# Queue order of expert weights, halved loads and a regrouped end in a two-layer mixture-of-experts kernel

## The chip, the cores and the metric

One core of a Trainium2 chip (trn2) runs the whole program. The metric is the device time of one execution in microseconds (us); of several executions the median counts. PE is the matrix engine (TensorE), DVE the vector engine, ACT the scalar engine, SP the engine whose only task here is to issue transfers (DMAs) from memory to the on-chip buffers.

## What is computed

Two decoder layers on 256 tokens of width 1024, all in float32. Each layer is a mixer (layer 0: sparse attention beside block attention; layer 1: stick-breaking attention), a layer norm, a mixture of 16 experts, and a second layer norm. The change touches the experts alone:

```python
def hierarchical_moe(x, w_grp, b_grp, w_rt, b_rt, w_gate, w_up, w_down):
    ...                      # two experts for each token, weights in combine
    def per_sequence(args):
        xs, cs = args
        h = jax.nn.silu(jnp.einsum('sd,edf->sef', xs, w_gate)) * jnp.einsum('sd,edf->sef', xs, w_up)
        return jnp.einsum('sef,efd->sd', h * cs[..., None].astype(h.dtype), w_down)
    return lax.map(per_sequence, (x, combine))

def reference(x, ...):
    for layer in range(DEPTH):
        ...
        x = layer_norm(DEEPNORM_ALPHA * x + mix, ln_mix_g[layer], ln_mix_b[layer])
        ffn = hierarchical_moe(x, ...)
        x = layer_norm(DEEPNORM_ALPHA * x + ffn, ln_ffn_g[layer], ln_ffn_b[layer])
    return x
```

An expert has 2 MB of gate and up weights (1024 x 512) and 1 MB of down weights (256 x 1024), so a layer reads 48 MB of expert weights.

## The kernel before

The 16 experts of a layer are worked through in seven units: `POS = [(0, 1), (2, 3), (4, 5), (6, 7), (16,), (8, 9, 10, 11), (12, 13, 14, 15)]`. Units 0 to 3 are pairs of experts with 64 token slots each, unit 4 takes overflow tokens, units 5 and 6 are four experts with 32 slots each. Places from 6 on are filled by the token counts at run time, and their weights are fetched by a register address (`expert`, a load of a register on SP the first time a place is asked for).

A unit passes through these steps, each a function: `gather(u)` picks its tokens into `xg` (L1201), `gate_up(u)` multiplies them with the gate and up weights, 8 chunks of 128 rows by 2 or 4 experts (L1234), `act_h` applies silu on ACT and the product on DVE (L1240, L1242), `tr_h` transposes the result on PE (L1249) and copies it to `hT` on ACT (L1250), `down(u)` multiplies with the down weights, two column halves of 512 (L1266), and splits each half into a high part (ACT, L190) and a low part (DVE, L198), and `scatter(u)` adds the rows back to the tokens in four accumulators `oacc[t][h]` (L1275). `scatter_end` (L1281) does the last scatters of units 5 and 6. The four experts of units 5 and 6 stand in four row strips ("lanes") of the matrix engine, so four products run side by side; each product of the program is two rows in the trace.

The steps of neighbouring units overlap; the order of the calls at the end of `moe_` is written by hand, and a scheduler that orders by its own estimates decides how the products of overlapping steps interleave on an engine. Each engine then works strictly in that order. `tc.issue_after(x)` tells the scheduler to place what follows behind instruction x.

Weights come through SP's one queue, in program order. A load at the head that waits for its buffer holds back all loads behind it. A load also waits until the eighth load before it has landed, since eight semaphores take turns. The buffers:

- six of 2 MB (`wtile`, pool `wp`) in rotation, for gate and up weights, mixer weights, and one pair of down weights (`w2`);
- four of 1 MB (`wd_tile`) in rotation for down weights;
- one of 1 MB (`wd_extra`), used for expert 4, then for the first expert of unit 5, then for the last expert of unit 6.

`load_gu(l, q)` loads the pair q as two loads, each four chunks of both experts; `load_gu_of(u, j)` loads piece j of a unit, one load for each expert; `load_d_at` and `load_d_of` load the 1 MB of down weights of one expert. After the last of them, in layer 0, come `wb` (2 MB of the next mixer's weights, L76) and the rows of gain and bias of the layer norm, `lngb` (two loads of 512 KB, L307).

The end of layer 0 is a layer norm by token halves t = 0, 1 (`ln_tile`): sums on DVE (L319, L321), the product with the gain on DVE (L347, needs the first `lngb`), two squares on ACT (L328), the root (L331 to L335), the last product (L356), transposes on PE (L284), copies to `xT` on ACT (L291), and then the first products of the next mixer, 16 rows for each half (L229). Thirty small products (L302) keep the matrix engine busy from the last scatter on.

## Time and profile before

| | us |
|---|---|
| median of 3 runs (539.48 to 541.42) | 541.22 |
| the profiled execution | 538.35 |
| its span, first to last instruction | 536.6 |
| PE busy | 503.1 |
| ACT busy | 221.9 |
| DVE busy | 289.4 |

The profiled execution is 2.9 us below the median of the three runs. What lies around its span is 1.75 us. The experts of layer 0 run from about 165 us to 276 us, those of layer 1 from about 412 us to 523 us, and the layer norm that ends the program follows. A sum over a stage has to be read in that stage: the matrix engine is busy 94% of the span, but the two ends of the expert stages hold most of what is left.

### The profile page before, as it was taken

To read this page: it belongs to the slowest core of one execution; us is meant where nothing else is said; L and a number is where in the kernel's file an instruction comes from. 1 tells how busy PE (TensorE), PEld (TensorE's weight loads), DVE (VectorE), ACT (ScalarE), POOL (GpSimd) and SP (SyncE) were. 2 spreads that over 40 slices of the span, in tenths; PEclk is the share of its full clock that TensorE was granted. 3 is DMA by queue.
4 is the path that set the end of the run, shared out by engine and by line. 5 is a ranking of instruction groups with operands and counts; after the bars stand their busy time and mean duration, and the time that the engine had idled before them with its cause. 6 is when DMAs were issued, how large, how long until landed. Compare 5 with 4: busy or idle time off the path is not lost.

```text
span 536.6 us, 8446 instructions
## 1 busy us (share of the span) xinstructions
PE 503.1 (94%) x3170; PEld 317.5 (59%) x3170; DVE 289.4 (54%) x828; ACT 221.9 (41%) x425; POOL 6.6 (1%) x18
## 2 busy tenths in 40 slices
PE   6998989999999999999989999999999999999980
PEld 3886666666676354543354997798677544363330
DVE  5587986957759732221158364555748861141116
ACT  5383635547647021221146237665847421131022
POOL 0000000000001000000000000000002000000000
PEclk9799989999999999999999999999999999999896
DMA  8999500007967899999998790002985599999952
GB/s 265 350 428 434 206 1 1 0 1 277 427 238 307 337 366 340 410 423 420 434 425 379 302 368 37 1 1 101 425 318 225 221 393 340 409 422 420 425 223 84
DMA packets 25247, 150.01 MB, mean 280 GB/s; under 512 B 3440, under 2 KB 3824, under 8 KB 14704
## 3 DMA queue, kind: packets, MB, share of 16 engines
q1 hardware_dynamic: 25200, 149.41, 69.8%
q8 instruction: 27, 0.44, 0.3%
q14 instruction: 20, 0.16, 0.1%
HBM read 148.35 MB, written 1.05 MB: 278 GB/s over the span
## 4 chain that ended last, share of the span: by engine, by line
PE 81%; DVE 8%; DMA 5%; ACT 4%; issue 1%; SPq 0%; ACTq 0%; DVEq 0%
PE pmt L1234 15%; PE pmt L1266 8%; PE pmt L1201 4%; PE acc L221 4%; DMA wb<-w1s 4%; PE acc L220 3%; PE acc L219 3%; PE acc L1275 3%; PE acc L373 3%; PE acc L371 3%; PE acc L372 3%; PE acc L229 3%; PE acc L243 2%; PE acc L241 2%; PE acc L242 2%; PE z L850 2%
## 5 line engine op out<-in xcount | busy, mean ns | idle before, releaser
L1234 PE MATMUL pmt<-wgu,xg 128*64 128x512 f32 (+1 forms) x512 | 93.5, 599 | 0.0
L193 DVE TENSOR_TENSOR wl<-wb,wh 128x512 fp32r<-128x512 f32 (+1 forms) x78 | 49.1, 661 | 22.4 <-ACT wh L190 22.3
L190 ACT ACTIVATE wh<-wb 128x1024 fp32r<-128x1024 f32 (+2 forms) x41 | 40.9, 1000 | 45.3 <-PE acc L220 21.3
L1234 PEld LDWEIGHTS pmt<-wgu,xg 128*64 128x64 f32 (+1 forms) x512 | 27.3, 124 | 53.5 <-issue 50.8
L1266 PE MATMUL pmt<-wd,hT 128*64 128x512 f32 (+1 forms) x256 | 54.6, 604 | 0.9 <-ACT hT L1250 0.9
L219 PE MATMUL acc<-wh,xhl 128*128 128x512 f32 (+1 forms) x112 | 45.9, 410 | 4.0 <-ACT wh L190 3.3
L221 PE MATMUL acc<-wl,xhl 128*128 128x512 f32 (+1 forms) x112 | 45.7, 414 | 3.2 <-DVE wl L193 3.2
L220 PE MATMUL acc<-wh,xhl 128*128 128x512 f32 (+1 forms) x112 | 45.1, 402 | 0.0
L198 DVE TENSOR_TENSOR yl<-pmt,yh 128x512 fp32r<-128x512 f32 x20 | 13.8, 690 | 49.1 <-ACT yh L190 49.1
L1242 DVE SCALAR_TENSOR_TENSOR hh<-pmt,cs,silu 128x256 f32<-128x256 f32 x12 | 5.8, 484 | 56.8 <-ACT silu L1240 56.8
L1240 ACT ACTIVATE silu<-pmt 128x256 f32<-128x256 f32 x12 | 4.6, 384 | 76.1 <-PE pmt L1234 76.1
L190 ACT ACTIVATE yh<-pmt 128x512 fp32r<-128x512 f32 x20 | 11.9, 597 | 57.5 <-PE pmt L1266 57.5
L1266 PEld LDWEIGHTS pmt<-wd,hT 128*64 128x64 f32 (+1 forms) x256 | 15.4, 124 | 27.2 <-issue 25.3
L221 PEld LDWEIGHTS acc<-wl,xhl 128*128 128x128 f32 x112 | 22.2, 199 | 9.3 <-DVE wl L193 4.0
L219 PEld LDWEIGHTS acc<-wh,xhl 128*128 128x128 f32 x112 | 22.4, 200 | 8.9 <-ACT wh L190 4.4
L1201 PEld LDWEIGHTS pmt<-Poh,xhl 128*128 128x128 f32 x192 | 24.5, 188 | 5.3 <-issue 3.2
L241 PE MATMUL acc<-xhl,wh 128*128 128x256 f32 x96 | 27.6, 287 | 0.0
L1201 PE MATMUL pmt<-Poh,xhl 128*128 128x256 f32 (+1 forms) x192 | 26.8, 293 | 0.3 <-DVE xg L1209 0.3
L243 PE MATMUL acc<-xhl,wl 128*128 128x256 f32 x96 | 27.0, 281 | 0.0
L242 PE MATMUL acc<-xhl,wh 128*128 128x256 f32 x96 | 26.8, 280 | 0.0
L373 PE MATMUL acc<-xol,oT 128*128 128x512 f32 x64 | 26.1, 412 | 0.0
L371 PE MATMUL acc<-xo,oT 128*128 128x512 f32 x64 | 25.9, 410 | 0.0
(367 smaller groups left out, 964.3 us busy)
## 6 DMA issues: line engine op xcount, KB each, us to landing
wd<-wd SPq DMA_DIRECT2D x34, 1024.0 KB, 11.0
wgu<-wgu SPq DMA_DIRECT2D x64, 512.0 KB, 11.6
wgu<-wgu SPq DMA_DIRECT2D x14, 2048.0 KB, 10.4
wb<-w1s SPq DMA_DIRECT2D x6, 2048.0 KB, 19.6
wo<-wo SPq DMA_DIRECT2D x4, 2048.0 KB, 16.9
wgu<-wgu SPq DMA_DIRECT2D x8, 1024.0 KB, 6.9
wb<-w SPq DMA_DIRECT2D x3, 2048.0 KB, 19.4
wb<-w SPq DMA_DIRECT2D x2, 1024.0 KB, 12.2
```

What stands on the lines that cost most here:

```text
L190: A.activation(dst_h, src, AF.Copy)
L193: V.tensor_tensor(dst_l[:, i], src[:, i], dst_h[:, i].bitcast(F32), OP.subtract)
L219: PE.matmul(a[t][:, :n], xh[:, cc, ts], wh[:, c, :n], start=(cc == 0), stop=False)
L220: PE.matmul(a[t][:, :n], xl[:, cc, ts], wh[:, c, :n], start=False, stop=False)
L221: PE.matmul(a[t][:, :n], xh[:, cc, ts], wl[:, c, :n], start=False, stop=(cc == NCH - 1))
L241: PE.matmul(o, wh[:, c, fs], xh[:, cc], start=(cc == 0 and f % 2 == 0), stop=False, skip_group_check=True)
L243: PE.matmul(o, wl[:, c, fs], xh[:, cc], start=False, stop=(cc == NCH - 1), skip_group_check=True)
L371: PE.matmul(a[t][h], oc[:, 0, ts], wh[:, hs], start=first, stop=False)
L373: PE.matmul(a[t][h], oc[:, 0, ts], wl[:, hs], start=False, stop=last)
L1201: PE.matmul(p[:, 0:w], src[:, t, c * 128:c * 128 + 128], P[:, t, u * 128:u * 128 + w], start=(t == 0 and src is xh), stop=(t == 1 and src ...
L1234: PE.matmul(pg[r, :], g[:, c, BASE[u] + r.start:BASE[u] + r.stop], ws[k, c], start=(c == 0), stop=(c == NCH - 1), tile_position=(0, r.start))
L1266: PE.matmul(y[r, :], hT[:, fc, r], wd[k][:, fc, h * 512:h * 512 + 512], start=(fc == 0), stop=(fc == 1), tile_position=(0, r.start))
```

## The change

Four edits, the same in both layers, since `moe_` is called for each.

1. The third pair (experts 4 and 5) is loaded by `load_gu(l, 2)`: two loads of four chunks of both experts, in place of one load for each expert. The down weights of expert 4 follow both.
2. `load_gu_of(5, 0)`, four loads of 512 KB, goes ahead of the down weights `load_d_at(2, 1)` and `load_d_of(3, 0)`.
3. The down weights of unit 6 are loaded by column halves: the first 512 columns of experts 0 to 3, then the last 512 columns of 0 to 3. The buffers are the same, and the last expert's is still `wd_extra`.
4. The scatters of unit 5 that stand at the end are placed behind the last gate product of unit 6, the last scatters of unit 6 behind its last down product, and their order is changed.

```diff
         weights, Am, seconds = router(lg)
         load_gu(l, 1)
-        wloads[l, 2, 0] = {}
-        for i in range(2):
-            w = chunks(wtile("wgu"))
-            SP.dma_start(w, io["wgu"][l * NE + 4 + i])
-            for c in range(NCH):
-                wloads[l, 2, 0][i, c] = w[:, c]
-            if i == 0:
-                load_d_at(2, 0, wd_extra())
+        load_gu(l, 2)
+        load_d_at(2, 0, wd_extra())
...
+        def load_d_half(u, i, wd, h):
+            hs = slice(h * 512, h * 512 + 512)
+            SP.dma_start(wd[:, :, hs], io["wd"][l * NE:(l + 1) * NE][ds(expert(POS[u][i]), 1)].rearrange("e p (f n) -> p (e f) n", f=2)[:, :, hs])
+            wloads.setdefault((l, u, 1), {})[i] = wd
...
-        def scatter_end(u1, u2):
-            for u, h, t in ((u2, 0, 0), (u1, 0, 1), (u1, 1, 1), (u2, 1, 0), (u2, 0, 1), (u2, 1, 1)):
-                for i in range(2):
-                    last["PE"] = PE.matmul(oacc[t][h], ...)
+        def scatter_end(u1, u2, down2):
+            for u, h, t in ((u1, 0, 1), (u1, 1, 1), (u2, 0, 0), (u2, 1, 0), (u2, 0, 1), (u2, 1, 1)):
+                with (tc.issue_after(down2) if u == u2 else nullcontext()):
+                    for i in range(2):
+                        last["PE"] = PE.matmul(oacc[t][h], ...)
...
         do_down(0)
+        load_gu_of(5, 0)
         load_d_at(2, 1, wd_tile())
         load_d_of(3, 0, wd_tile())
-        load_gu_of(5, 0)
...
-        load_d_of(6, 0, w2[:, 0])
-        load_d_of(6, 1, w2[:, 1])
+        w6 = [w2[:, 0], w2[:, 1]]
+        load_d_half(6, 0, w6[0], 0)
+        load_d_half(6, 1, w6[1], 0)
...
-        load_d_of(6, 2, wd_tile())
+        w6.append(wd_tile())
+        load_d_half(6, 2, w6[2], 0)
...
-        load_d_of(6, 3, wd_extra())
+        w6.append(wd_extra())
+        load_d_half(6, 3, w6[3], 0)
+        for i in range(4):
+            load_d_half(6, i, w6[i], 1)
...
         hid[6], _ = act_h(6, pg)
+        gate6 = last["G"]
         do_tr(6)
-        do_scatter(5, [0])
+        with tc.issue_after(gate6):
+            do_scatter(5, [0])
...
-        scatter_end(5, 6)
+        with tc.issue_after(gate6):
+            scatter_end(5, 6, last["D"])
```

Here `last["G"]` and `last["D"]` are the latest gate product and down product. What the scheduler makes of it shows in the order of the instructions on the engines. Line numbers of the changed kernel differ by a few (L1233 is L1234 of before, L1265 is L1266, L1274 is L1275, L1248 is L1249).

On PE at the end of the experts, the rows from the last down products of unit 5 (`pmt<-wd,hT`) on; `pmt<-wgu,xg` are gate products of unit 6, `acc<-yh,ST` and `acc<-yl,ST` scatters of unit 5, `pmt<-identf,hh` the transposes of unit 6. Before:

```order
L1266 MATMUL pmt<-wd,hT 32x512 x12
L1234 MATMUL pmt<-wgu,xg 32x512
L1275 MATMUL acc<-yh,ST 128x512
L1275 MATMUL acc<-yl,ST 128x512
L1234 MATMUL pmt<-wgu,xg 32x512
L1275 MATMUL acc<-yh,ST 128x512
L1275 MATMUL acc<-yl,ST 128x512
L1281 MATMUL acc<-yh,ST 128x512
L1281 MATMUL acc<-yl,ST 128x512
L1281 MATMUL acc<-yh,ST 128x512
L1281 MATMUL acc<-yl,ST 128x512
L1234 MATMUL pmt<-wgu,xg 32x512 x14
```

and in the changed kernel:

```order
L1265 MATMUL pmt<-wd,hT 32x512 x12
L1233 MATMUL pmt<-wgu,xg 32x512 x16
L1274 MATMUL acc<-yh,ST 128x512
L1274 MATMUL acc<-yl,ST 128x512
L1274 MATMUL acc<-yh,ST 128x512
L1274 MATMUL acc<-yl,ST 128x512
L1281 MATMUL acc<-yh,ST 128x512
L1248 MATMUL pmt<-identf,hh 128x128 x2
L1281 MATMUL acc<-yl,ST 128x512
L1281 MATMUL acc<-yh,ST 128x512
L1281 MATMUL acc<-yl,ST 128x512
L1265 MATMUL pmt<-wd,hT 32x512 x16
```

The 16 gate products now follow the down products without a scatter between them, and the eight scatters stand between the gates and unit 6's down products, the transposes among them; the count of each kind is the same.

On ACT in the layer norm that ends layer 0, from the root of the first token half (L332) on; `acc,lnst<-xn,lnst` is a square of one column half, `xT<-pmt` the copies of the first token half's transposes. Before:

```order
L332 ACTIVATE lnst<-lnst 128x1
L291 ACTIVATE xT<-pmt 128x4x128 x2
L328 ACTIVATE acc,lnst<-xn,lnst 128x512 x2
L331 ACTIVATE lnst<-lnst 128x1
L332 ACTIVATE lnst<-lnst 128x1
L190 ACTIVATE xhl<-xT 128x4x128 x2
```

and in the changed kernel:

```order
L332 ACTIVATE lnst<-lnst 128x1
L328 ACTIVATE acc,lnst<-xn,lnst 128x512
L291 ACTIVATE xT<-pmt 128x4x128 x2
L328 ACTIVATE acc,lnst<-xn,lnst 128x512
L331 ACTIVATE lnst<-lnst 128x1
L332 ACTIVATE lnst<-lnst 128x1
L190 ACTIVATE xhl<-xT 128x4x128 x2
```

The first square of the second token half has moved ahead of the two copies of the first token half. In layer 1 ACT's order is that of before, and DVE's is in both layers.

On SP at the end of layer 0's expert loads, from the last loads of unit 6 on (`ISA`, which sets the register address, stands ahead of each). Before:

```order
L1182 ISA
L1182 DMA wd<-wd 128x2048
L76 DMA wb<-w1s 128x4096
L307 DMA lngb<-lng 128x1024
L307 DMA lngb<-lnb 128x1024
```

and in the changed kernel (the first `wd` row here is the first half of the last expert, into `wd_extra`; three first halves stand ahead of it):

```order
L1181 DMA wd<-wd 128x2x512
L1181 ISA
L1181 DMA wd<-wd 128x2x512
L1181 ISA
L1181 DMA wd<-wd 128x2x512
L1181 ISA
L1181 DMA wd<-wd 128x2x512
L1181 ISA
L1181 DMA wd<-wd 128x2x512
L76 DMA wb<-w1s 128x4096
L307 DMA lngb<-lng 128x1024
L307 DMA lngb<-lnb 128x1024
```

Behind the load into `wd_extra` there now stand four more halves before `wb` and the rows of the layer norm.

## Rows read from the trace of the kernel before

**Rows 1.** The page: span, busy times, the DMA engines' busy tenths in 40 slices of 13.4 us, and the chain that ended last, by engine.

```profile
span 536.6 us, 8446 instructions
PE 503.1 (94%) x3170; PEld 317.5 (59%) x3170; DVE 289.4 (54%) x828; ACT 221.9 (41%) x425; POOL 6.6 (1%) x18
DMA  8999500007967899999998790002985599999952
PE 81%; DVE 8%; DMA 5%; ACT 4%; issue 1%; SPq 0%; ACTq 0%; DVEq 0%
```

**Rows 2.** PE in order of time, end of the experts of layer 1: start, duration (us), line, operation, number of rows in the trace, and in brackets the idle time before and what ended it. The first row is the first scatter behind unit 5's down products.

```profile
508.11 0.50 PE L1275 MATMUL acc<-yh,ST 128*128 128x512 f32 x1
...
509.15 1.05 PE L1234 MATMUL pmt<-wgu,xg 128*32 128x512 f32 x2
...
511.72 3.63 PE L1234 MATMUL pmt<-wgu,xg 128*32 128x512 f32 x28
516.35 0.44 PE L1249 MATMUL pmt<-identf,hh 128*128 128x128 f32 x2 [1.00 <-DVE hh L1242]
517.26 3.68 PE L1266 MATMUL pmt<-wd,hT 128*32 128x512 f32 x32 [0.47 <-ACT hT L1250]
520.87 2.37 PE L1281 MATMUL acc<-yb,ST 128*128 128x512 f32 x8
```

**Rows 3.** The same of layer 0, with the first products of the next mixer.

```profile
260.81 0.50 PE L1275 MATMUL acc<-yh,ST 128*128 128x512 f32 x1
...
264.42 3.63 PE L1234 MATMUL pmt<-wgu,xg 128*32 128x512 f32 x28
...
269.96 3.68 PE L1266 MATMUL pmt<-wd,hT 128*32 128x512 f32 x32 [0.47 <-ACT hT L1250]
...
280.61 1.13 PE L284 MATMUL pmt<-identf,xn 128*128 128x128 f32 x8
281.90 7.13 PE L229 MATMUL acc<-wb,xT 128*128 128x512 f32 x16 [0.15 <-ACT xT L291]
```

**Rows 4.** Waits of the issuing engine SP: what waited, for what, us in total, times, longest. First row: from 186 to 204 us (layer 0, the down weights of expert 5 at the head). Second: from 246 to 262 us (layer 0, the load into `wd_extra`). Third: from 493 to 509 us (the same of layer 1).

```profile
SPq L1015 <- PE pmt L1266: 7.8, 1, 7.8
...
SPq L1182 <- PE pmt L1266: 5.8, 1, 5.8
...
SPq L1182 <- PE pmt L1266: 5.1, 1, 5.1
```

**Rows 5.** Stretches: from:to and length (us), busy time and count of PE, PE weight load, DVE, ACT, POOL, then the granted clock as a share, the DMA engines' busy share and GB/s. In the last row only the output's rows of 2 KB are under way; in the fourth, pieces of 4 and 8 KB.

```profile
192.00:193.00 1.00, 1.00 (x10) 1.00 (x9) 0.67 (x2) 0.33 (x2) 0.00 (x0) 1.00 0.76 156
...
195.90:250.60 54.70, 53.24 (x348) 24.55 (x347) 12.03 (x30) 10.18 (x22) 0.00 (x0) 1.00 1.00 393
...
444.00:494.90 50.90, 50.64 (x348) 23.86 (x347) 11.41 (x29) 9.32 (x20) 0.00 (x0) 1.00 1.01 397
...
462.00:482.00 20.00, 19.74 (x161) 11.06 (x156) 6.28 (x15) 4.96 (x11) 0.00 (x0) 1.00 1.02 423
...
531.00:532.00 1.00, 0.00 (x0) 0.00 (x0) 0.90 (x2) 0.00 (x0) 0.00 (x0) 0.50 1.01 391
```

**Rows 6.** Single loads: start and duration of the issue on SP, and below it KB and us from issue to landing. First pair: the load into `wd_extra` of layer 0; second: the gain of the layer norm that ends layer 0; third: the load into `wd_extra` of layer 1. The last three rows are loads issued while no other load was outstanding, at 423.98, 370.79 and 313.73 us.

```profile
260.10 0.33 SPq L1182 DMA_DIRECT2D wd<-wd  x1
wd<-wd SPq DMA_DIRECT2D x1, 1024.0 KB, 8.9
261.01 0.37 SPq L307 DMA_DIRECT2D lngb<-lng  x1
lngb<-lng SPq DMA_DIRECT2D x1, 512.0 KB, 14.1
507.40 0.33 SPq L1182 DMA_DIRECT2D wd<-wd  x1
wd<-wd SPq DMA_DIRECT2D x1, 1024.0 KB, 9.7
wgu<-wgu SPq DMA_DIRECT2D x1, 1024.0 KB, 5.2
wd<-wd SPq DMA_DIRECT2D x1, 1024.0 KB, 4.8
wgu<-wgu SPq DMA_DIRECT2D x1, 2048.0 KB, 8.7
```

**Rows 7.** DVE and ACT in order of time in the layer norm that ends layer 0: the product with the gain (first token half), the sum of the second token half, then on ACT the copies to `xT` of the first token half and the first square of the second.

```profile
276.70 1.28 DVE L347 SCALAR_TENSOR_TENSOR lnu<-xn,lnst,lngb 128x1024 f32<-128x1024 f32 x1
...
282.22 0.21 DVE L321 TENSOR_SCALAR lnst<-lnst 128x1 f32<-128x1 f32 x1
...
281.25 1.13 ACT L291 ACTIVATE xT<-pmt 128x512 f32<-128x512 f32 x2 [2.31 <-DMA wb<-w1s]
282.47 0.69 ACT L328 ACTIVATE acc<-xn,lnst 128x512 f32<-128x512 f32 x1
```

**Rows 8.** Stretches again, columns as in rows 5: unit 5's down products with unit 6's gate products in layer 0, the same in layer 1, and inside the latter the part at the lower clock.

```profile
252.00:260.70 8.70, 8.70 (x67) 2.92 (x66) 0.03 (x1) 0.60 (x1) 0.00 (x0) 1.00 1.03 425
...
497.80:508.10 10.30, 10.30 (x67) 3.13 (x66) 0.12 (x1) 0.60 (x1) 0.00 (x0) 0.85 1.03 427
...
497.50:500.90 3.40, 3.40 (x12) 0.73 (x11) 0.00 (x0) 0.00 (x0) 0.00 (x0) 0.50 1.02 417
```

More of the change, by code (lines that the diff above doesn't have):

```diff
@@ L1233, in gate_up @@
                 for k, r in lanes(u):
-                    PE.matmul(pg[r, :], g[:, c, BASE[u] + r.start:BASE[u] + r.stop], ws[k, c],
-                              start=(c == 0), stop=(c == NCH - 1), tile_position=(0, r.start))
+                    last["G"] = PE.matmul(pg[r, :], g[:, c, BASE[u] + r.start:BASE[u] + r.stop], ws[k, c],
+                                          start=(c == 0), stop=(c == NCH - 1), tile_position=(0, r.start)).ins
             return pg
@@ L1265, in down @@
                     for k, r in lanes(u):
-                        PE.matmul(y[r, :], hT[:, fc, r], wd[k][:, fc, h * 512:h * 512 + 512],
-                                  start=(fc == 0), stop=(fc == 1), tile_position=(0, r.start))
+                        last["D"] = PE.matmul(y[r, :], hT[:, fc, r], wd[k][:, fc, h * 512:h * 512 + 512],
+                                              start=(fc == 0), stop=(fc == 1), tile_position=(0, r.start)).ins
                 ys.append(split_y(y, dst[h]))
@@ L1275, in scatter @@
                         PE.matmul(oacc[t][h], ST[:, u, t * 128:t * 128 + 128], ys[h][i], start=(u == 0 and i == 0), stop=False)
-        def scatter_end(u1, u2):
-            for u, h, t in ((u2, 0, 0), (u1, 0, 1), (u1, 1, 1), (u2, 1, 0), (u2, 0, 1), (u2, 1, 1)):
-                for i in range(2):
-                    last["PE"] = PE.matmul(oacc[t][h], ST[:, u, t * 128:t * 128 + 128], ys[u][h][i], start=False, stop=(u == u2 and i == 1)).ins
+        def scatter_end(u1, u2, down2):
+            for u, h, t in ((u1, 0, 1), (u1, 1, 1), (u2, 0, 0), (u2, 1, 0), (u2, 0, 1), (u2, 1, 1)):
+                with (tc.issue_after(down2) if u == u2 else nullcontext()):
+                    for i in range(2):
+                        last["PE"] = PE.matmul(oacc[t][h], ST[:, u, t * 128:t * 128 + 128], ys[u][h][i], start=False, stop=(u == u2 and i == 1)).ins
         def over_gate_up(gx):
```

## The prediction

> **What bounds the kernel now.** I read the page first. PE is busy 94% of the span, and the chain that ended last is PE for 81% of its length [rows 1]. The DMA engines' tenths stand at 9 for long stretches [rows 1], so loads could bound too; which of the two does, the stretches tell. Through most of the expert stage PE works 53.24 of 54.70 us in layer 0 and 50.64 of 50.90 us in layer 1 [rows 5]. Weights therefore arrive in time there, and an earlier weight can give at most the 1.46 and 0.26 us that PE is idle. What is left lies at the two ends of the expert stages. In order of time, PE finishes the gate products of unit 6 at 511.72 + 3.63 = 515.35, stands idle 1.00 us for the product on DVE and 0.47 us for the copy on ACT, and starts the down products at 517.26 [rows 2]. Layer 0 shows the same step, with the same durations, 247.30 us earlier [rows 3]. I then read SP's waits: the queue's head is blocked 7.8 us in layer 0 by the down weights of expert 5, and in both layers, 5.8 and 5.1 us, by the load into `wd_extra` [rows 4].
>
> The profiled execution took 538.35 us, a span of 536.6 [rows 1] and 1.75 around it. It lies 2.9 us below the median of the runs, so I make the sum against 538.35 and add 2.9 at the end. Half a per cent, about 2.7 us, is what a measurement of this kernel can tell from no change.
>
> **Edits 1 and 2: nothing on the path.** Unit 5's first loads no longer stand behind the head that is blocked 7.8 us. While it is, the DMA engines fall to 156 GB/s [rows 5], against 423 when they flow. The loads that follow land some 5 us earlier. PE has work there (53.24 of 54.70 us), and that work is the cover; were it gone, 1.46 us would be the most to win. A loss needs a load that comes later than its product; the down weights that are put back have until their unit's down products, and PE is fed through the stretch. I take 0. The edits do have one effect: everything ahead of the last down weights is read earlier, so the queue will have run dry when `wd_extra` comes free.
>
> **Edit 4: the down products of unit 6 could start 3.45 us earlier.** Before, PE needs 515.35 - 508.11 = 7.24 us from the first scatter to the last gate product [rows 2]. Without scatters among them, the 30 rows recorded take 3.9 us at the rate of the unbroken part, 28 in 3.63 us. Four products run side by side, and the two rows more can fill sets that the break leaves half empty, so I take 3.65 us: the gates end near 511.75. From there to the down products the chain stays as it is (silu, product, transposes, copy): 517.26 - 515.35 = 1.91 us. The eight scatters take about 0.25 us each (six of them fill the 1.52 us from 509.15 + 1.05 to 511.72), 2.0 us in all, against 1.47 us of idle time; but a first few of them start while the last gate products drain, so I charge 0.15 us. The down products could start at 513.8 in layer 1 and, by the same sum, 266.5 in layer 0, where they now start at 517.26 and 269.96.
>
> **Edit 3: the weights take half of that back.** The down products last 3.68 us [rows 2]; by column halves, the second half starts 1.84 us after the first, at 515.65 and 268.35. It needs the last half-load, and that one stands in the queue behind the first half of the last expert, which waits for `wd_extra`. The buffer comes free with unit 5's down products at 260.1 and 507.4 [rows 6]; the order of PE ahead of that is unchanged, so that moment (call it E) stays. Four second halves that have their buffers already are stuck behind it. At E five loads of 512 KB go into an idle queue:
>
> - Starting again: a lone load of 1 MB lands after 5.2 us or 4.8 us [rows 6]; flowing at 423 GB/s [rows 5] it takes 2.5. So 2.7 us of delay; bounds 2.3 us (from 4.8) and 3.7 (a lone 2 MB load, 8.7 less 5.0).
> - Five halves: their rows are 2 KB long. The nearest row is the output with the same length, 391 GB/s against 423 for longer ones [rows 5]; I take 387, 1.355 us for each, 6.8 in all.
> - Stragglers: a burst ends with a us at 156 GB/s [rows 5]; I add 0.3 us, bounds 0 and 0.6.
>
> The last half lands at E + 9.8: 269.9 and 517.2. Now the whole load, issued at the same moments, lands after 8.9 and 9.7 us, at 269.0 and 517.1 [rows 6]. So although the down weights are split, their last part comes no sooner. PE waits about 1.6 us in the middle of the down products and ends 1.84 us after the landing: 519.05 where it now ends at 517.26 + 3.68 = 520.94. **Layer 1 gains 1.85 us**, and the last scatters, the same eight rows in 2.37 us, follow as before. In layer 0 the experts end at 271.75 instead of 273.64.
>
> The Trainium skill, "DMA: Bandwidth & Descriptors", section "Latency and other measured facts", gives about 0.6 us to the first byte of a load from SP's queue. By that alone the last half would land at E + 7.4 and the wait would be almost gone; the lone loads here, 2.3 to 3.7 us longer than their bytes, do not agree, and I go by them.
>
> **Layer 0: the layer norm gives it back.** Its gain row stands behind the last halves and `wb`. It lands now 6.1 us behind the last down weights (261.01 + 14.1 = 275.1, less 269.0 [rows 6]), so at 276.0 in the changed kernel. The product with the gain starts now at 276.70 [rows 7], 3.06 us after the experts' end; that would make 274.8, but it must wait for the landing, and starts at 276.05. Of 1.9 us, 0.65 is left. Next, ACT's order has changed: the first square of the second token half is ahead of the copies to `xT`. The square needs the sum of that half, which DVE gives at 282.22 + 0.21 = 282.43 [rows 7], 281.8 after the shift. The square takes 0.69 us, so the copies start at 282.5 instead of 281.25. The first products of the next mixer start 0.65 us behind the copies (281.90 now [rows 3]): 283.15. That is **1.3 us later than before**. From there PE runs its 16 rows without a gap [rows 3], so the delay is carried on. If the square were not in the way, layer 0 would gain the 0.65.
>
> **Sum:** +1.3 - 1.85 = -0.55, that is 537.8 for the profiled execution and **540.7 us** as a median. The terms of the landing count in both layers (layer 0 through the gain row), each us twice: the short bounds of restart and stragglers, 0.7 us together, make -1.95; the long ones, 1.3 us, make +2.05.
>
> **Rivals.**
>
> *The halves are in time.* If the last half lands by E + 8, PE doesn't wait: layer 1 gains the whole 3.45 us, and with E + 7.4 the gain row lands 2.4 us earlier than forecast, so layer 0 comes out at +1.3 - 2.45 = -1.15. Sum -4.6, 536.6 us. For it speaks that the queue need not be quite dry at E: the earlier loads might still flow, and then the 2.7 us of restart fall away. Against it that three second halves less stand ahead of the blocked head than before, 1.5 MB, some 3.7 us of queue.
>
> *A loss of clock (the slower side).* Layer 0 gets new idle time on PE: between the transposes (281.74 now, 0.65 earlier in the changed kernel) and L229 about 2.1 us, where 0.15 stood [rows 3]; and some 1.2 us more ahead of the transposes, since the small products that keep PE busy end with the experts 1.9 us earlier and the transposes only 0.65. In layer 1 a stretch at 0.50 of the clock begins at 497.5 [rows 8]; by that, 10.30 us went for the same 67 rows that take 8.70 in layer 0 [rows 8]. One such stretch, 1.6 us, makes +1.05 and 542.3; two make +2.65 and 543.9. Slower is decided from the first stretch on. Against it: the idle time of 1.00 and 0.47 us in both ends now costs no clock in what follows at the same durations [rows 2, 3]. The dip at 497.5 may also not return, which gives 1.6 us: -2.15, 539.1 us.
>
> *Short loads don't flow.* Of the lone loads, the second MB costs 8.7 less 4.8 to 5.2, about 3.7 us [rows 6], not 2.5: halves at that rate take 1.85 us each, 2.5 us more per layer, in both layers: +4.4 and 545.6 us. Slower by over half a per cent from about 1.7 us a half on. Against it, loads of 512 KB and 1 MB one behind the other make 423 GB/s [rows 5]. The Trainium skill, same page, section "Bandwidth", has the rule to batch loads to 1 MiB or more for at least 75% of the peak, which speaks against halves; the stretch at 423 GB/s does not bear it out for a full queue.
>
> That the edits don't do what they say is ruled out by the order of the instructions.
>
> **How the numbers follow.** Chances: forecast 0.54; halves in time 0.21; loss of clock 0.15, a third of it with two stretches or with a late landing besides; short loads 0.05; the dip gone 0.05. The forecast, one stretch and the dip lie within half a per cent. Faster by over half a per cent 0.23, which is the halves in time and a little of the dip with a short restart; slower 0.11, from two stretches, short loads, and the long end of the forecast with one stretch; the same 0.66. The forecast's own range is 539.3 to 542.8. The range reaches from the halves in time, 536.5, to two stretches, 543.9; outside it lie the short loads and what joins several cases.
>
> **What would show it.** In the changed kernel: PE in layer 1 from its first down product of unit 6 at about 513.8, with an idle time of 1.6 us in the middle of the 32 rows, ended by a DMA of `wd`, and the same in layer 0; a stretch of some us just before E with the DMA engines near 0 GB/s; the product with the gain ended by the landing of `lngb`; the copies to `xT` behind the square, L229 near 283.2 on the old scale with PE idle 2 us ahead of it, and the granted clock of that stretch at 1.00; SP's 7.8 us at the head gone with no change of PE's share behind it. I am wrong if the last half lands more than 1 us away from E + 9.8, if the clock halves at L229, or if the gain row isn't what the layer norm waits for.

## The result

The changed kernel takes 541.56 us (median of 20 runs, 537.99 to 545.50), the kernel before 538.34 us (median of 20 runs, 533.74 to 541.80). The ratio is 1.010, with a 95% interval of 1.007 to 1.013: **slower by about 5.4 us** (3.8 to 7.0), where the forecast was 0.55 us faster. The ratio is formed from the fast runs of both kernels alone; the two medians make 1.006 and the two means of all 20 runs 1.008. The median of 541.22 us that stands in the table above came from three runs and was 2.9 us too high; over 20 runs the median is that of the profiled execution (538.35). So the 2.9 us added at the end of the sum were not there, and the 540.7 us of the forecast lie near the measured time by chance.

From the page of the changed kernel: span, busy times, and the granted clock in tenths.

```profile
span 542.8 us, 8478 instructions
PE 510.1 (94%) x3170; PEld 322.9 (59%) x3170; DVE 289.8 (53%) x828; ACT 222.0 (41%) x425; POOL 6.6 (1%) x18
PEclk9896899999999999999998999999999999999996
```

The page shows little: PE's share is 94% as in [rows 1], and the 7.0 us of more busy time are no more work (x3170 in both): 3.8 us of them stand in the down products (58.4 us on this page, 54.6 on that of before), whose rows are drawn out while weights are awaited, and the rest comes with stretches at a lower clock.

The clock is also why the two timelines can't be laid on each other from zero. In the first 90 us PE has stretches at half the clock that differ from one execution to the next. Below, the same two stretches in the kernel before, in the changed kernel, and in a second profile of the changed kernel (columns as in rows 5; the clock is the third number from the end):

```profile
44.40:58.00 13.60, 12.55 (x119) 8.50 (x121) 10.82 (x37) 7.99 (x22) 0.00 (x0) 1.00 0.81 346
77.60:81.00 3.40, 3.40 (x10) 2.55 (x10) 3.40 (x11) 1.06 (x1) 0.00 (x0) 0.51 0.00 0
```
```profile
44.40:58.00 13.60, 13.60 (x70) 9.62 (x69) 7.20 (x26) 4.32 (x12) 0.00 (x0) 0.50 0.81 346
77.60:81.00 3.40, 1.04 (x5) 0.70 (x5) 2.94 (x9) 0.43 (x2) 0.00 (x0) 1.00 0.00 0
```
```profile
44.40:58.00 13.60, 12.56 (x115) 8.51 (x117) 10.81 (x37) 7.90 (x22) 0.00 (x0) 1.00 0.86 364
77.60:81.00 3.40, 3.40 (x9) 2.66 (x9) 3.25 (x12) 1.06 (x1) 0.00 (x0) 0.51 0.00 0
```

So everything below is counted from E, the issue of the load into `wd_extra`, as in the prediction. E is a moment of PE (unit 5's last down products). Where the early stretches are alike, E is alike: 260.10 before [rows 6] and 260.17 in the second profile of the changed kernel.

```profile
260.17 0.54 SPq L1181 DMA_DIRECT2D wd<-wd  x1
```

That is the answer on edits 1 and 2: up to E of layer 0 they neither win nor cost anything.

**Layer 1, from E = 512.20.** PE in order of time, from the gate products on, and then, from the view of waits, what the weight loads of the down products waited for from 511 to 527 us (us, times, longest):

```profile
512.42 4.00 PE L1233 MATMUL pmt<-wgu,xg 128*32 128x512 f32 x27
...
518.62 2.76 PE L1265 MATMUL pmt<-wd,hT 128*32 128x512 f32 x18
521.91 1.04 PE L1265 MATMUL pmt<-wd,hT 128*32 128x512 f32 x2 [0.53 <-DMA wd<-wd]
523.27 1.05 PE L1265 MATMUL pmt<-wd,hT 128*32 128x512 f32 x2 [0.32 <-DMA wd<-wd]
524.62 1.90 PE L1265 MATMUL pmt<-wd,hT 128*32 128x512 f32 x10 [0.29 <-DMA wd<-wd]
526.45 2.21 PE L1281 MATMUL acc<-yb,ST 128*128 128x512 f32 x8
```
```profile
PEld pmt L1265 <- DMA wd<-wd: 3.9, 3, 1.4
```

The down products start at E + 6.42, against E + 9.86 before [rows 2, 6]: edit 4 brings its 3.4 us. They then last 7.9 us instead of 3.68, since three halves come late, and the last scatters begin at E + 14.25 instead of E + 13.47. The gain is gone and 0.6 to 0.8 us more.

**Layer 0, from E = 261.90.** PE, then DVE's product with the gain, then ACT:

```profile
268.35 2.96 PE L1265 MATMUL pmt<-wd,hT 128*32 128x512 f32 x20
...
272.91 1.90 PE L1265 MATMUL pmt<-wd,hT 128*32 128x512 f32 x10 [0.29 <-DMA wd<-wd]
...
282.47 1.25 PE L353 MATMUL pmt<-lnst,identf 128*128 128x256 f32 x4 [2.22 <-DVE lnst L335]
...
286.62 8.86 PE L229 MATMUL acc<-wb,xT 128*128 128x512 f32 x16 [1.20 <-ACT xT L291]
```
```profile
279.60 1.28 DVE L347 SCALAR_TENSOR_TENSOR lnu<-xn,lnst,lngb 128x1024 f32<-128x1024 f32 x1 [1.89 <-DMA lngb<-lng]
...
285.27 0.69 ACT L328 ACTIVATE acc<-xn,lnst 128x512 f32<-128x512 f32 x1 [3.53 <-DVE lnst L321]
286.00 1.06 ACT L291 ACTIVATE xT<-pmt 128x512 f32<-128x512 f32 x2
```

The product with the gain waits 1.89 us for its load and starts at E + 17.7 (before, E + 16.6). The copies to `xT` stand behind the square. L229 starts at E + 24.7 (before E + 21.8), and its 16 rows take 8.86 us instead of 7.13 [rows 3]. In all, the copy that follows them (L870) is 4.65 us later. With the 0.6 us of layer 1 that makes 5.3 us, within the 3.8 to 7.0 us measured.

One difference lies ahead of E and is not in this sum: the stretch at 0.50 that begins at 497.5 before [rows 8] is in none of the three profiles of the changed kernel (clock 1.00 over the 12.8 us ahead of E, 0.87 before). Four of the other profiles have such a stretch, at the same place in layer 0 or layer 1, so it seems to come and go; if every execution of the kernel before had it, the sum would be 1.6 us less, 3.7 us.

### The profile page after: what moved, and what is told of

Read it like the earlier page. It is cut to its first block, busy times and chain, and to the rows that moved or that the text cites. A ratio compares the mean times of both kernels' runs of the same rounds, so it can differ in the third digit from the quotient of the medians.

```text
span 542.8 us, 8478 instructions
## 1 busy us (share of the span) xinstructions
PE 510.1 (94%) x3170; PEld 322.9 (59%) x3170; DVE 289.8 (53%) x828; ACT 222.0 (41%) x425; POOL 6.6 (1%) x18
## 4 chain that ended last, share of the span: by engine, by line
PE 80%; DVE 9%; DMA 5%; ACT 3%; issue 1%; SPq 1%; ACTq 0%; DVEq 0%
PE pmt L1233 15%; PE pmt L1265 7%; PE pmt L1200 4%; PE acc L221 4%; PE acc L219 4%; PE acc L220 4%; PE acc L1274 3%; PE acc L373 3%; PE acc L229 3%; PE acc L371 3%; PE acc L372 3%; DMA lngb<-lng 2%; PE acc L243 2%; PE acc L241 2%; PE acc L242 2%; DMA wd<-wd 2%
## 5 line engine op out<-in xcount | busy, mean ns | idle before, releaser
L1233 PE MATMUL pmt<-wgu,xg 128*64 128x512 f32 (+1 forms) x512 | 92.0, 594 | 0.0
L1233 PEld LDWEIGHTS pmt<-wgu,xg 128*64 128x64 f32 (+1 forms) x512 | 28.5, 123 | 53.1 <-issue 51.7
L1265 PE MATMUL pmt<-wd,hT 128*64 128x512 f32 (+1 forms) x256 | 58.4, 599 | 1.7 <-DMA wd<-wd 1.7
L219 PE MATMUL acc<-wh,xhl 128*128 128x512 f32 (+1 forms) x112 | 46.6, 416 | 1.5 <-ACT wh L190 0.9
L220 PE MATMUL acc<-wh,xhl 128*128 128x512 f32 (+1 forms) x112 | 45.8, 409 | 0.0
L198 DVE TENSOR_TENSOR yl<-pmt,yh 128x512 fp32r<-128x512 f32 x20 | 13.8, 690 | 47.5 <-ACT yh L190 47.5
L1265 PEld LDWEIGHTS pmt<-wd,hT 128*64 128x64 f32 (+1 forms) x256 | 15.4, 123 | 31.4 <-issue 23.9
```

The costliest lines, as they stand in the source:

```text
L219: PE.matmul(a[t][:, :n], xh[:, cc, ts], wh[:, c, :n], start=(cc == 0), stop=False)
L220: PE.matmul(a[t][:, :n], xl[:, cc, ts], wh[:, c, :n], start=False, stop=False)
L1233: last["G"] = PE.matmul(pg[r, :], g[:, c, BASE[u] + r.start:BASE[u] + r.stop], ws[k, c], start=(c == 0), stop=(c == NCH - 1), tile_positio ...
L1265: last["D"] = PE.matmul(y[r, :], hT[:, fc, r], wd[k][:, fc, h * 512:h * 512 + 512], start=(fc == 0), stop=(fc == 1), tile_position=(0, r.s ...
```

## Experiments

Each ratio is to the kernel before, with its 95% interval. The table counts from E: where the last down weights land, where unit 6's down products end, and two sums to hold against the ratio, the change up to L870 (the copy behind L229's first 16 rows, 28.97 us after E before) and up to the end of layer 1's last scatter (15.84 us after E before). Each row is one profile. What lies behind that scatter is left out (13.3 us before and with edit 4 alone, 13.8 to 14.5 in the others; the cause is not shown).

| kernel | ratio | last landing, layers 0, 1 | down end | L870, change | layer 1, change |
|---|---|---|---|---|---|
| before | | 8.9, 9.7 | 13.6, 13.5 | | |
| changed | 1.010 (1.007 to 1.013) | 11.0, 12.4 | 12.9, 14.3 | +4.65 | +0.62 |
| changed, again | 1.012 (1.004 to 1.019) | 11.4, 12.4 | 13.3, 14.4 | +4.54 | +0.69 |
| without edit 3 | 0.988 (0.982 to 0.994) | 5.8, 8.5 | 10.1, 12.1 | -3.43 | -1.55 |
| without edit 3, again | 0.989 (0.984 to 0.995) | 5.0, 8.7 | 10.1, 12.4 | -3.42 | -1.33 |
| edit 3 alone | 1.014 (1.009 to 1.020) | 10.9, 12.3 | 16.1, 16.1 | +4.39 | +2.45 |
| edit 4 alone | 1.002 (0.998 to 1.006) | 9.3, 9.4 | 13.0, 13.0 | -0.66 | -0.67 |
| edits 1 and 2 alone | 1.002 (0.998 to 1.006) | 5.3, 8.2 | 13.5, 13.5 | -0.02 | -0.04 |
| edits 3 and 4 | 1.011 (1.006 to 1.016) | 11.1, 13.3 | 13.1, 15.2 | +5.32 | +1.53 |
| last expert's halves last | 0.993 (0.989 to 0.998) | 8.3, 9.0 | 10.2, 11.3 | +0.04 | -2.37 |
| ACT's order of before | 1.001 (0.996 to 1.007) | 11.8, 11.9 | 13.7, 13.8 | +1.33 | +0.10 |
| gain ahead of `wb` | 1.006 (1.002 to 1.010) | 11.4, 11.7 | 13.3, 13.6 | -0.33 | -0.07 |
| halves by rows | 1.010 (1.006 to 1.015) | 11.3, 12.6 | 13.3, 14.6 | +4.47 | +1.07 |
| three repairs together | 0.985 (0.981 to 0.989) | 7.3, 8.6 | 10.1, 11.0 | -3.22 | -2.73 |

### Which edit costs it

Edit 3 taken out, which is `load_d_of` for all four experts of unit 6, and all else as changed:

```diff
...
-        load_d_half(6, 3, w6[3], 0)
-        for i in range(4):
-            load_d_half(6, i, w6[i], 1)
+        load_d_of(6, 3, wd_extra())
```

> The change without edit 3: the down weights of unit 6 are loaded whole again, the load into `wd_extra` is the last one before `wb`. Theory A (the halves behind the blocked head cost the time): only one load of 1 MB is left to go into an idle queue at E, and lone loads of 1 MB landed after 4.8 to 5.2 us, so it is there at about E + 5.0, before the down products can start at E + 6.4. The 3.45 us of edit 4 are won whole in layer 1. In layer 0 the gain row lands at about E + 11.2, ahead of its use, ACT's order is that of before, and 3.3 us are won. Ratio to before about 0.9875. Theory B (edits 1, 2 or 4 themselves, or the clock, cost the time): still 1.00 or above.

Measured 0.988, and 0.989 in a second run beside the repaired kernel:

> The change without edit 3 once more, beside the repaired one on the same chip. Its first profile gives, from E on, 3.4 us won in layer 0 and 1.0 to 1.5 us in layer 1: ratio 0.991 to 0.992.

PE of that second run, in both layers, and the loads issued at E (258.75 and 500.92):

```profile
265.19 3.68 PE L1259 MATMUL pmt<-wd,hT 128*32 128x512 f32 x32
...
277.12 7.13 PE L229 MATMUL acc<-wb,xT 128*128 128x512 f32 x16
...
507.34 1.93 PE L1259 MATMUL pmt<-wd,hT 128*32 128x512 f32 x12
509.66 3.62 PE L1259 MATMUL pmt<-wd,hT 128*32 128x512 f32 x20 [0.38 <-DMA wd<-wd]
```
```profile
wd<-wd SPq DMA_DIRECT2D x1, 1024.0 KB, 5.0
...
wd<-wd SPq DMA_DIRECT2D x1, 1024.0 KB, 8.7
```

In layer 0 the whole load is there after 5.0 us, the down products run in one piece from E + 6.44, and L229 starts at E + 18.4, 3.4 us earlier than before. In layer 1 the queue has other loads left at E, the load takes 8.7 us, and one wait is left: 1.3 to 1.6 us are won there, not the 3.45 us expected. Theory A holds but for that: the other three edits are worth 1.1%, and edit 3 costs 2%.

Edit 3 alone on the kernel before:

> The kernel before with edit 3 alone. The queue is not dry when `wd_extra` comes free (before, the loads ahead land until E + 6.4), so no restart: the last half should land about 0.6 us later than the whole load did, E + 9.5, while the second column half of the down products, starting at E + 11.7, does not wait. What is left is ACT's order in the layer norm of layer 0, which is that of the changed kernel here: the copies to `xT` behind a square, 1.9 us. Theory A: ratio 1.0035 without a loss of clock. If the clock is lost because L229 starts after about 2 us of idle time, 1.006 to 1.008. Rival C (halves are slow in themselves, restart or not): last half at E + 11 or later, 1.005 and more from the waits alone.

Measured 1.014, worse than theory A gives, and not by waiting for loads:

```profile
268.69 2.76 PE L1272 MATMUL pmt<-wd,hT 128*32 128x512 f32 x18 [0.47 <-ACT hT L1256]
271.39 0.51 PE L1287 MATMUL acc<-yb,ST 128*128 128x512 f32 x1
272.12 0.97 PE L1287 MATMUL acc<-yb,ST 128*128 128x512 f32 x3 [0.22 <-DVE yb L198]
273.01 1.92 PE L1272 MATMUL pmt<-wd,hT 128*32 128x512 f32 x14
275.67 1.46 PE L1287 MATMUL acc<-yb,ST 128*128 128x512 f32 x4 [0.73 <-ACT yb L190]
```

With halves in the queue, the scheduler puts four scatters between the down products; no wait for `wd` is left, but the second half starts 2.5 us later and its split no longer hides behind anything. My expectation did not have this order. The last half lands at E + 10.9 and E + 12.3, not at E + 9.5: on the landings rival C is the nearer, though nothing waits for them here. In the changed kernel edit 4 forbids it (`issue_after` the last down product), so the two edits are not additive. In ACT's order the 1.9 us are there (L229 at 4.15 us behind L353, 2.23 before).

Edit 4 alone, and edits 1 and 2 alone:

> The kernel before with edit 4 alone. The down products could start 3.45 us earlier in both layers, but need the whole last load, which lands at E + 8.9 in layer 0 and E + 9.7 in layer 1 as before: 1.0 us won in layer 0, 0.2 us in layer 1. Ratio 0.998. If edit 4 itself costs something (theory B), 1.00 or more, with the gate products' row or the chain behind them longer than 3.65 and 1.91 us.

> The kernel before with edits 1 and 2 alone: no order of PE, ACT or DVE differs from before. The last load lands at about E + 5 instead of E + 8.9, and nothing waited for it: ratio 1.000 by theory A. Rival D (the earlier weights do fill idle time in the middle, or the new order at the start of the experts costs some): 0.997 to 1.004, with the difference in time before E.

Both 1.002, no change that can be told from none. With edit 4 alone the down products start at E + 6.4, take 12 rows and then wait for the whole load, which lands at E + 9.3 in both layers (8.9 and 9.7 were expected); the two sums make -1.3 us, 0.9975, just below the interval. With edits 1 and 2 alone the load lands at E + 5.3 in layer 0 and nothing else moves. So by the times neither is worth anything without the other: edit 4 needs the weights earlier, edits 1 and 2 need someone who waits for them.

### A dry queue, or the place in it

The edits 3 and 4 without 1 and 2:

> The change without edits 1 and 2: the halves and the gate order stay, the earlier loads stand as before, so that the queue has more left when `wd_extra` comes free. If the queue running dry is what makes the last half late (the step of the forecast that took the restart as a term), the first half lands without a restart, the last at E + 10 or earlier in both layers, and the ratio falls to 1.000 to 1.003. If the place of the four halves behind the blocked load is what counts, dry or not, the last half lands at E + 10.9 to 12.4 as in the changed kernel and the ratio stays at 1.008 to 1.011.

Measured 1.011: the place counts. Below, us from issue to landing in layer 0 of the first half of the last expert, of the load behind it, and of the last half (issued at 257.01, 257.76 and 259.98):

```profile
wd<-wd SPq DMA_DIRECT2D x1, 512.0 KB, 4.4
wd<-wd SPq DMA_DIRECT2D x1, 512.0 KB, 6.4
wd<-wd SPq DMA_DIRECT2D x1, 512.0 KB, 8.2
```

The load ahead of them lands at E + 3.1 here, so the first half follows it without a pause, at E + 4.4. The next one still comes 2.7 us later, the last at E + 11.1. In layer 1 the loads ahead take until E + 5.9, the halves follow 1.3 to 1.8 us apart, and the last lands at E + 13.3. That edits 1 and 2 let the queue run dry is true in layer 0, but it is not what costs.

The queue order that leaves one half behind the blocked load:

```diff
-        load_d_half(6, 3, w6[3], 0)
-        for i in range(4):
-            load_d_half(6, i, w6[i], 1)
+        for i in range(3):
+            load_d_half(6, i, w6[i], 1)
+        for h in range(2):
+            load_d_half(6, 3, w6[3], h)
```

> The changed kernel with one thing different: the last halves of experts 0 to 2 stand ahead of both halves of the last expert, so that only one half is stuck behind the load that waits for `wd_extra`. Theory A: the two halves land at E + 4 and E + 7 to 7.4, the second column half starts at E + 8.3 and doesn't wait: 2.7 us won in layer 0, 4.1 us in layer 1, the gain row lands at about E + 13 and the layer norm does not wait for it, 4.5 us won at its first product in all. ACT's order stays. 8.6 us faster than the changed kernel, ratio to before 0.994, and 0.991 if the clock at L229 comes back too. Theory C (halves are slow whatever stands where): second half of the last expert at E + 10 or later, 1.005 or more.

Measured 0.993, 9 us faster than the changed kernel by one move in the queue. PE, layer 1:

```profile
510.35 4.91 PE L1265 MATMUL pmt<-wd,hT 128*32 128x512 f32 x32
```

4.91 us for the down products instead of 7.9. The last half lands at E + 9.0 there, and at E + 8.3 in layer 0, 4.0 us behind the half ahead of it. One part of the expectation missed: the layer norm still waits for its gain row, which lands at E + 14.7 instead of E + 13. Two more profiles of this kernel (below) spread the change up to L870 from -1.30 to +1.02 us.

### The layer norm of layer 0

ACT's order of before, by placing the squares of the second half behind the copies (`with tc.issue_after(last["X"])` around `ln_rstd`, where `X` is the copy of L291):

> The changed kernel with the squares of the second token half placed behind the copies to `xT` of the first in the layer norm that ends layer 0, which is ACT's order of before; nothing else moves. L229 should start 2.2 us behind L353 as before, instead of 4.15: 1.9 us won, ratio 1.006 to 1.0065. If the idle time of 1.2 us ahead of L229 is what cost the clock, another 1.7 us, 1.003.

The two loads of gain and bias ahead of `wb`:

```diff
+        gb = load_ln(2 * l + 1, wk.tile([128, 2, D], F32, name="lngb", tag="Poh"))
         if before_end:
             before_end(-1)
-        gb = load_ln(2 * l + 1, wk.tile([128, 2, D], F32, name="lngb", tag="Poh"))
```

> The changed kernel with the two loads of the layer norm's gain and bias ahead of `wb` in the queue; this also brings back ACT's order of before in that layer norm. The gain row lands at E + 12.3 instead of E + 17.6, and its product starts with the end of the sums, 1.85 us earlier; with ACT's order 3.75 us won, ratio 1.003, and 1.000 if the clock at L229 comes back. Against the run with ACT's order alone 1.85 us. `wb` lands 2.5 us later, at E + 18.8, ahead of L229 by some 3 us. If the sums, not the gain row, hold the product, no difference to the run with ACT's order alone.

The first gives 1.001, below the interval of the changed kernel, the second 1.006, which overlaps it; which of the two is better the times don't tell. The twelve runs of the first lie from 532 to 543 us, so its 1.001 is loose; its two sums, 1.4 us, give 1.003. The rows are sharper. ACT's order alone:

```profile
284.14 1.11 PE L353 MATMUL pmt<-lnst,identf 128*128 128x256 f32 x4 [1.73 <-DVE lnst L335]
286.37 7.13 PE L229 MATMUL acc<-wb,xT 128*128 128x512 f32 x16 [0.15 <-ACT xT L291]
```

L229 is 2.23 us behind L353, as before. With the gain ahead, DVE no longer waits for it:

```profile
279.50 0.21 DVE L321 TENSOR_SCALAR lnst<-lnst 128x1 f32<-128x1 f32 x1
279.75 1.29 DVE L347 SCALAR_TENSOR_TENSOR lnu<-xn,lnst,lngb 128x1024 f32<-128x1024 f32 x1
```

It starts at E + 16.3 instead of E + 17.7. By the sums that kernel should be at 0.999, and its measured interval begins at 1.002; what makes the rest was not found.

### The clock at L229

> The changed kernel once more. Its first profile gives, from E on, +2.9 us until L229 in layer 0 and +0.8 us until the last low part of unit 6 in layer 1, and 1.7 us that 16 rows of L229 took longer at the lower clock: 5.4 us together, the whole of the measured 1.010. If the clock falls at L229 in every execution, 1.010 again and a stretch at 0.50 begins there again. If that was chance, its profile shows 1.00 there, and the ratio is between 1.007 and 1.010.

> One more profile of the changed kernel. If the loss of clock at L229 belongs to its idle time there (2.2 us ahead of L353 and 1.2 us ahead of L229), a stretch at 0.50 begins within 5 us of L353 here too, as in both profiles so far; if it is chance, it is at 1.00.

Both profiles show the loss again: 8.83 us for the 16 rows, the second with a clock of 0.81 over 8.85 us, so 3 of 3 profiles of the changed kernel. The kernel with halves by rows (below) and edits 3 and 4 without 1 and 2 show it too (8.83 and 9.16 us). Of the queue order with the last halves last there are three profiles, of edit 3 alone two:

> One more profile of the queue order with the last expert's halves last. Its first profile had the same idle times ahead of L353 (1.79 us) and L229 (2.07 us) as two profiles of the changed kernel (1.74 and 2.07, 1.70 and 2.08), and no loss of clock where those lost 1.7 us. If idle times of this length cost the clock by chance, the loss shows in some of these looks: 16 rows of L229 in 8.8 us instead of 7.13. If something else of the changed kernel brings it, 7.13 again.

> The same as the look before it: 8.8 us for 16 rows of L229 if the loss is a matter of chance at these idle times, 7.13 us if it belongs to something else in the changed kernel.

> One more profile of edit 3 alone, with 0.47 us of idle time ahead of L353 and 2.07 us ahead of L229: 16 rows of L229 in 7.13 us if it takes the idle time ahead of L353 too to lose the clock, 8.8 us in a share of looks if the 2.07 us alone do.

The first profile of that queue order, and the second:

```profile
276.00 1.11 PE L353 MATMUL pmt<-lnst,identf 128*128 128x256 f32 x4 [1.79 <-DVE lnst L335]
...
280.15 7.13 PE L229 MATMUL acc<-wb,xT 128*128 128x512 f32 x16 [2.07 <-ACT xT L291]
```
```profile
279.54 1.11 PE L353 MATMUL pmt<-lnst,identf 128*128 128x256 f32 x4 [1.09 <-DVE lnst L335]
...
283.68 8.83 PE L229 MATMUL acc<-wb,xT 128*128 128x512 f32 x16 [2.07 <-ACT xT L291]
```

With more idle time the first keeps 2.4 GHz, and the second, with less, falls to 1.2 (columns as in rows 5; the clock is 0.81 over its 16 rows):

```profile
283.68:292.51 8.83, 8.83 (x18) 3.85 (x19) 3.48 (x9) 3.53 (x8) 0.00 (x0) 0.81 1.00 428
```

The third profile of that order (0.47 and 2.07 us) and both of edit 3 alone (0.47 and 2.07) keep it; so does ACT's order alone (1.73 and 0.15). Where PE stood idle in both places (1.09 to 2.45 us ahead of L353, 1.20 to 2.08 us ahead of L229), 6 of 7 profiles lost 1.7 us or more; where in one of them only, none of those shown.

The idle time ahead of L229 is not always part of it, though. In the first profile of the changed kernel the clock is down before L229 begins; over the 4.91 us up to L229 (from 281.71) it is 0.66:

```profile
281.71:286.62 4.91, 2.95 (x12) 2.33 (x12) 4.68 (x11) 1.38 (x5) 0.00 (x0) 0.66 1.00 427
```

It is 1.00 until 283.3 (E + 21.4) and 0.50 from there on, while the products of L353 and L284 run. In that of edits 3 and 4 the fall comes at E + 22.4, again ahead of L229. These two have the longest idle times ahead of L353, 2.22 and 2.45 us. In the other four the clock falls within 1 us of L229's start. That idle time goes with the loss is likely; which of the two it takes, and why one profile of seven kept the clock, stays open.

### Short pieces

The halves cut by rows of the down weights, so that pieces are 4 KB:

```diff
-            SP.dma_start(wd[:, :, hs], ...[:, :, hs])
+            SP.dma_start(wd[:, h:h + 1, :], ...[:, h:h + 1, :])
```

> The changed kernel with its half-loads cut by rows of the down weights instead of columns: pieces of 4 KB instead of 2 KB, the same 512 KB each, the same order and the same place in the queue (every down product then needs both halves, so PE waits at once; only the landings are read). If the short pieces are what makes the second half land 2.9 to 3.8 us after the first on a queue that starts again, it lands 1.3 us after it here, and the last at about E + 9.3. If it is the start of the queue itself, the second half lands 2.9 us or more after the first here too, and the last at E + 10.5 or later.

The first, second and last of the five, issued at 255.24, 255.78 and 257.36:

```profile
wd<-wd SPq DMA_DIRECT2D x1, 512.0 KB, 3.6
wd<-wd SPq DMA_DIRECT2D x1, 512.0 KB, 5.4
wd<-wd SPq DMA_DIRECT2D x1, 512.0 KB, 9.2
```

The second lands 2.3 us after the first (3.3 in layer 1), the last at E + 11.3 and E + 12.6. The second is between the two expectations, the last is as late as with 2 KB. So the length of the pieces is not what makes the loads behind E late.

### The repairs together

Last expert's halves last, ACT's order of before, gain ahead of `wb`:

> The changed kernel with the three repairs together: both halves of the last expert behind the other six, ACT's order of before, gain and bias ahead of `wb`. From E on: down products end at E + 10.2 in layer 0 and E + 11.3 in layer 1; the gain row lands at about E + 9.5; the low part that follows L229 at E + 25.6, where it was E + 28.97 before; end of layer 1's stage 1.5 us earlier than before. 4.9 us in all, ratio 0.991; against the run with that queue order alone 3.4 us or 0.006 less. If the layer norm has another limit than the gain row and ACT's order, 0.993 to 0.994.

Measured 0.985 (median 528.24 us): faster than both kernels, 2.5% ahead of the changed one, a larger gain than the expected 0.991; its two sums, -5.95 us, give 0.989, the upper end of its interval. PE, layer 0 and layer 1:

```profile
268.79 3.66 PE L1265 MATMUL pmt<-wd,hT 128*32 128x512 f32 x32
...
280.96 7.13 PE L229 MATMUL acc<-wb,xT 128*128 128x512 f32 x16 [0.15 <-ACT xT L291]
...
511.37 4.54 PE L1265 MATMUL pmt<-wd,hT 128*32 128x512 f32 x32
```

With E at 262.38 and 504.94, the down products take 3.66 us in layer 0 and 4.54 in layer 1, and L229 has neither the idle time nor the loss of clock. Whether it beats the change without edit 3 (0.989) can't be told: the intervals overlap. Its landing in layer 1 is at E + 8.6 like that of the whole load, but the first column half can start without it.

## Why the prediction was wrong

**What held.** PE is the bound through the stages, and edits 1 and 2 are worth nothing by themselves: SP's wait of 7.8 us for the down weights of expert 5 is 1.1 us in the changed kernel, and PE's busy time from 195.9 to 250.6 is 53.31 us in its second profile, 53.24 before. Edit 4: gates done 3.7 us earlier, down products at E + 6.4. Halves that flow land 1.3 to 1.4 us apart, as 1.36 was put. The halves behind the blocked load, the wait in the middle of the down products, the gain row as the next limit and ACT's order at 1.9 us were all there, where the prediction put them.

**The step that failed first** is the last term of the landing, "stragglers" at 0.3 us with a bound of 0.6. The first half came as worked out: E + 4.04 and E + 4.36 against 2.7 + 1.36 = 4.06. But the second came 2.9 to 3.0 us after it, not 1.36 (up to 3.8 in the other two profiles), and in layer 1 the third 2.3 us after that. Where 0.3 us were put, the loads behind the first lost 1.5 us in layer 0 and 2.6 us in layer 1 (there the first was 0.3 us late besides), so the last half lands at E + 11.0 and E + 12.4 instead of E + 9.8. Stretches of the DMA engines show where it lies, 264 to 268 and 268 to 272 in layer 0, 514 to 520 and 520 to 524 in layer 1:

```profile
264.00:268.00 4.00, 4.00 (x24) 2.05 (x17) 0.58 (x2) 0.63 (x2) 0.00 (x0) 1.00 0.86 248
268.00:272.00 4.00, 3.73 (x23) 0.91 (x22) 0.69 (x1) 2.02 (x3) 0.00 (x0) 1.00 1.08 399
514.00:520.00 6.00, 6.00 (x44) 2.71 (x37) 0.87 (x2) 2.05 (x3) 0.00 (x0) 1.00 0.94 261
520.00:524.00 4.00, 3.15 (x14) 0.43 (x6) 0.69 (x1) 0.60 (x1) 0.00 (x0) 1.00 1.04 405
```

For 4 to 6 us the engines are busy 86 to 94% of the time and move 248 to 261 GB/s, then 399 to 405. The row at 156 GB/s [rows 5] was read as the end of a burst; it stands where loads start again, behind the issue at 191.59 that ends SP's wait: the us after it has 213 GB/s, and 198 to 200 have 287, where the rest has some 420. That is 1.1 and 0.6 us of flow lost, so a term of 1 to 2 us could have been read there. I priced a start as a delay of the first load alone.

Each us counts in both layers, as the prediction says. In layer 1 it turns -1.85 into +0.6. In layer 0 the gain row lands at E + 17.6 instead of E + 15.9, and the product with the gain starts 1.1 us later than before instead of 0.65 earlier.

**The second miss** is the clock at L229, set down as a rival with a chance of 0.15. It came in every profile of the changed kernel and cost 1.7 us. The idle times are near those of the forecast: 2.1 us ahead of L229 in two of the three profiles (2.07 and 2.08; 1.20 in the first, where the clock fell earlier), and ahead of L353 1.2 to 1.8 us more than the 0.46 of before (2.22, 1.74, 1.70). The chance was too low: it leaned on idle times of 1.00 and 0.47 us that cost nothing, which are shorter than these.

From -0.55: 1.7 us for the gain row, 2.4 us in layer 1 and 1.7 us for the clock make +5.3. One slip besides: the long end of the forecast's own range is 541.25 + 2.05 = 543.3 us, not 542.8.

**Halves in time** did not come: it would have needed E + 8. **Short loads don't flow** came near in size (by it the last half lands at E + 12.3) but not in cause: the rate is low behind E alone, with 4 KB pieces too, and recovers. So the Trainium skill's rule on loads of 1 MiB ("DMA: Bandwidth & Descriptors", section "Bandwidth") would have pointed the right way here, and the whole loads are 2% faster; but by the table the gain comes from their place, since the halves in another order do about as well (0.993, and 0.985 with two repairs besides).

Of the prediction's other signs, one was off: in layer 1 the queue was not dry at E, since three halves landed at E - 1.2, E + 0.05 and E + 1.4.

## What to carry to other kernels

In a queue that issues in order, a split load is not only smaller pieces: whatever stands behind a piece whose buffer is not yet free becomes as late as that buffer. Put the pieces with free buffers ahead of the blocked one; here that one move turned a loss of 1% into a gain of 0.7%, and with two repairs next to it into 1.5%. Edits that each show nothing in the times alone (weights earlier, products earlier) can be worth 1% together, so before one is judged ask which of them is the other's limit.

## What the runs showed of the hardware

- In layer 0 of every profile with halves, the load behind the one that is issued at E lands 2.3 to 4.0 us after it instead of 1.3, with the queue empty or not, with pieces of 2 or 4 KB, while in the changed kernel's profile the engines are busy 86% of the time and move 248 GB/s. In layer 1 it is 1.3 to 3.8 us, with 1.3 in the two kernels whose other loads still land beyond E + 5 (last halves last, three repairs). The cause stays open.
- Of seven profiles with idle times of 1.09 to 2.45 us ahead of L353 and 1.20 to 2.08 us ahead of L229, six fell from 2.4 to 1.2 GHz, two of them before the second idle time; one, with 1.79 and 2.07 us, did not. A loss cost 1.7 to 2.0 us for 16 rows.
- The same early part of the program runs at half the clock for different times from one execution to the next: in the stretches shown 3.4 us in one and 13.6 us in another. The runs of one kernel go along with it: of the 20 of the changed kernel the fastest (537.99 us) had a mean granted clock of 0.984, the slowest (545.50 us) one of 0.970. E of layer 0 lies between 255.2 and 263.5 us in the profiles, which is why both kernels had to be compared from a moment that both share.
